# One down-projection sum per head, both branches' rows in one order on GpSimd, and piece two's token copies later: a hybrid decoder layer on one Trainium2 core

## The chip, the cores and the metric

The kernel runs on one core of one Trainium2 chip. The metric is device time in microseconds (us) of the whole program, less being better. An execution taken by the hardware profiler lies beside the timed runs; it gives when each engine was busy, what each instruction waited for, and which clock TensorE was granted. The engines are PE (TensorE), DVE (VectorE), ACT (ScalarE), POOL (GpSimd) and SP (SyncE, which here only issues DMAs). Each engine works its own instructions strictly in the order in which they were compiled: an instruction that waits holds everything behind it on that engine.

## The reference, cut to what matters

One layer, sequence 1024 plus 16 meta tokens, width 1024, all in float32. A token mixer has two parallel branches, gated linear attention (GLA, 4 heads) and mLSTM (4 heads), whose outputs are gated and merged; then comes a gated feed-forward network (FFN) with a causal convolution.

```python
proj = h @ w_in + b_in                        # q, k, v, gates of both branches
o_gla = head_rms(gla_chunked(...)) * silu(g_r)
o_ml  = head_rms(mlstm_chunked(...)) * sigmoid(m_o)
y = sigmoid(gate_a) * (o_gla @ w_branch_gla) + sigmoid(gate_b) * (o_ml @ w_branch_ml)
h = h + y @ w_out
u = causal_dwconv(rms_norm(h) @ w_up)
h = h + (silu(gate) * up) @ w_down
```

## The kernel before

Float32 operands are split on the chip into a high and a low part (ACT copies the high part, DVE subtracts it to get the low one), and each product is three matmuls: high x high, high x low, low x high. The large products of the gates and of the FFN use a Strassen-like scheme with seven block products instead of eight (`piece`), for which sums of token blocks and of weight blocks are made beforehand. The work around the change runs in four stages, in order of time.

**Heads (to about 680 us).** The loop at L950 goes over eight heads `s` (0 to 3 GLA, 4 to 7 mLSTM). Its main thread is the projections on PE (`value_proj`, `key_query_proj`); each of their steps calls `advance` (L931), which moves one generator of `closing` and one of `side` by a step. `side` holds `gla(s)` or `mlstm(s)`, the head's own recurrence. It ends in `rstd_of` (L88), whose power is taken on POOL (L93, tile `rs{s}r`). Its closing generator, `post(s)` (L558), scales the eight output blocks with that root on ACT (L563), transposes them on PE (L572), and stores two rows `of` to `oscm` or `oscg`. For s from 3 to 6, `post` then calls `token_sums(s - 3)` (POOL sums of token blocks, L464 and L469, stored by SP to `tsc`) and several `half_sums`.

`half_sums` (L478) is one of 22 pieces that make sums of w_down's blocks for the FFN's last product, long before they are needed. It takes one tile `ts`, loads 2 x 256 KB into it (L482, issued by POOL), makes four differences on POOL (L485) and stores two blocks to `tdn` (L487, POOL again). In the heads its tile is `gst` of pool `wp`, with one buffer, shared with `token_sums`' tile `tx` and with the rows `gb` of `merge_gate_b`. Heads make 2 + 3 + 3 of the 22, the gates 6, the first branch 3, the second branch 5.

**Gates (about 680 to 970 us).** `token_blocks` (L1071) loads the four token sums `T1` to `T4` from `tsc` with SP, in two pieces of columns (`W0` and the rest), and after each piece's loads come its splits on ACT (L1081) and DVE (L1082). Two further products, `merge_gate_b` for `COVER`, run on PE meanwhile. Then 13 pairs of gate products (L1124) run in two pieces each; pairs from 8 on also call `half_sums` (L1145) on tile `o0`. `gate_finish` multiplies a gate with a stored head output and stores the result to `otd`. The last plain product, `END`, is gate row 7 (`pe`), whose row `gb` goes to `gsc["b"]`.

**Branches (about 975 to 1200 us).** The first loop (L1206) makes `bg` = o_gla @ w_branch_gla in eight column tiles: `load_o("g")` (L1161) loads eight rows `ogL` of 513 KB with POOL, each split into `ogH` and `ogL` by ACT (L1171) and DVE (L1172); `merge_tile` (L1200) loads the gate rows `yg` with POOL; ACT takes their sigmoid (L1210), and DVE multiplies (L1213). At its second step it calls `load_o("m")`, which loads `omL` with SP, and three `half_sums`. The second loop (L1229) makes `bm` in eight tiles: it loads the row `sb` from `gsc["b"]` with SP (L1234), in two alternating tiles, ACT takes its sigmoid (L1235), DVE multiplies and adds (L1240, L1241), and while pieces are left each step ends in one `half_sums`, on the tile of the gate row that it has just used up.

**The rest:** the output product, the FFN's up products (with the convolution) and its down product.

The order on each engine is made by a compiler with a list scheduler: among the instructions that its own model calls ready it takes the one of highest priority, where priority is the order of the program, moved ahead by `hp(n)` blocks. So an instruction can be queued ahead of its place in the program. `tc.issue_after(x)` keeps the block's instructions on x's engine behind x, without a wait.

## Time and profile before

| | us |
|---|---|
| median of three runs | 1978.77 (1975.70 to 1982.41) |
| profiled execution | 1985.01 |
| its span, first to last instruction | 1983.3 |
| PE busy in it | 1883.7 |
| DVE busy | 1196.9 |
| ACT busy | 853.8 |
| POOL busy | 390.9 |

PE is busy for 95% of the span. A page of the profile gives each engine's busy time; the view of waits gives, for an engine and a line, who ended its idle time, with the total, the number of times and the longest; a timeline row gives start, duration, engine, line, operation, output<-inputs, shapes and count, and in brackets the idle time of the engine just before it and what ended it. SPq and ACTq rows are DMA issues.

### The profile page before, as it was taken

What the parts mean: (1) busy time and instruction counts of PE and PEld (TensorE: products, weight loads), DVE (VectorE), ACT (ScalarE), POOL (GpSimd) and SP (SyncE); (2) the same over time, 40 slices, a digit from 0 to 9 for tenths busy, and PEclk for the clock granted to TensorE, in tenths of its full rate; (3) what the DMA queues carried; (4) which work ended last, traced back from release to release, by engine and by line L of the source; (5) the groups of instructions that cost most, each with busy time, mean ns of one, the idle gap of its engine ahead of it and who ended that gap; (6) DMA issues with size and microseconds to landing.
All of it is one profiled execution on the core that took longest, in us unless ns stands there. A gap on an engine that the chain in (4) does not pass through costs nothing. (4 is left out here: it accounts for less than half of the span.)

```text
span 1983.3 us, 32663 instructions
## 1 busy us (share of the span) xinstructions
PE 1883.7 (95%) x13377; PEld 1799.7 (91%) x13377; DVE 1196.9 (60%) x1775; ACT 853.8 (43%) x1369; POOL 390.9 (20%) x425
## 2 busy tenths in 40 slices
PE   8999999999697989999869999999999999999998
PEld 8999989999686989999869999999999999987776
DVE  6555745655342255656251344788787878786867
ACT  5355554635333443432151123554444434354663
POOL 3101101142443001114340230012222222200000
PEclk8999999999898989999979999999999999999999
DMA  5111111143342547566871363333334333378794
GB/s 161 33 36 56 35 44 56 50 135 83 115 125 86 138 118 181 142 168 182 247 260 56 112 207 109 116 121 108 102 109 131 107 107 108 112 265 302 286 378 158
DMA packets 222593, 270.03 MB, mean 136 GB/s; under 512 B 13486, under 2 KB 176832, under 8 KB 222443
## 3 DMA queue, kind: packets, MB, share of 16 engines
q1 hardware_dynamic: 203771, 207.29, 33.8%
q0 software_dynamic: 14528, 50.39, 8.3%
q10 hardware_dynamic: 4144, 10.26, 1.5%
q8 instruction: 105, 1.72, 0.4%
q14 instruction: 45, 0.37, 0.1%
HBM read 198.33 MB, written 69.57 MB: 135 GB/s over the span
## 5 line engine op out<-in xcount | busy, mean ns | idle before, releaser
L485 POOL TENSOR_TENSOR ts<-ts 128x256 f32<-128x256 f32 x88 | 75.9, 866 | 69.2 <-DMA ts<-in_ffn_w_down_dram 66.7
L1188 PE MATMUL bg<-ogH,wH_bg 128*128 128x342 f32 x192 | 63.2, 330 | 24.3 <-ACT ogH L1171 24.3
L1372 POOL TENSOR_TENSOR SB<-SA,rg 128x512 f32<-128x512 f32 x20 | 32.1, 1604 | 237.1 <-issue 114.1
L201 PE MATMUL pv<-wH_mv,xH 128*128 128x256 f32 x256 | 75.5, 295 | 0.1
L201 PE MATMUL pv<-wH_gv,xH 128*128 128x256 f32 x256 | 75.3, 294 | 0.0
L1459 PE MATMUL po<-wH_wo,yH 128*128 128x256 f32 x256 | 72.6, 284 | 0.1
L201 PE MATMUL pv<-wL_mv,xH 128*128 128x256 f32 x256 | 72.5, 283 | 0.0
L201 PE MATMUL pv<-wH_mv,xL 128*128 128x256 f32 x256 | 72.5, 283 | 0.0
L1459 PE MATMUL po<-wL_wo,yH 128*128 128x256 f32 x256 | 71.9, 282 | 0.3 <-DVE wL_wo L107 0.3
L201 PE MATMUL pv<-wH_gv,xL 128*128 128x256 f32 x256 | 72.0, 281 | 0.0
L201 PE MATMUL pv<-wL_gv,xH 128*128 128x256 f32 x256 | 71.9, 281 | 0.0
L1459 PE MATMUL po<-wH_wo,yL 128*128 128x256 f32 x256 | 71.7, 281 | 0.0
L1407 DVE SCALAR_TENSOR_TENSOR cv<-u,fc,cv 128x1024 f32<-128x1024 f32 x44 | 65.3, 1485 | 0.4
L1188 PE MATMUL bg<-ogL,wH_bg 128*128 128x342 f32 x192 | 63.2, 330 | 0.3 <-DVE ogL L1172 0.3
L1188 PE MATMUL bg<-ogH,wL_bg 128*128 128x342 f32 x192 | 63.0, 328 | 0.0
L1354 POOL TENSOR_TENSOR A<-u2raw,A 128x512 fp32r<-128x512 f32 x20 | 44.0, 2198 | 93.0 <-ACT A L1353 93.0
L690 POOL TENSOR_TENSOR pk<-pk,kT 128x256 f32<-128x256 f32 (+1 forms) x24 | 29.5, 1231 | 163.5 <-ACT pk L688 163.5
L1188 PE MATMUL bm<-omH,wH_bm 128*128 128x342 f32 x192 | 61.4, 320 | 0.0
L1188 PE MATMUL bm<-omH,wL_bm 128*128 128x342 f32 x192 | 61.3, 319 | 0.0
L1188 PE MATMUL bm<-omL,wH_bm 128*128 128x342 f32 x192 | 61.2, 319 | 0.0
L1188 PEld LDWEIGHTS bg<-ogH,wH_bg 128*128 128x128 f32 x192 | 37.8, 197 | 24.9 <-ACT ogH L1171 24.9
L482 POOL DMA_DIRECT2D ts<-in_ffn_w_down_dram x44 | 32.0, 732 | 122.8 <-DVE yM L1244 84.3
(750 smaller groups left out, 7487.2 us busy)
## 6 DMA issues: line engine op xcount, KB each, us to landing
gw<-in_w_in_dram SPq DMA_DIRECT2D x26, 512.0 KB
ts<-in_ffn_w_down_dram POOLq DMA_DIRECT2D x44, 256.0 KB, 3.9
tdn<-ts POOLq DMA_DIRECT2D x44, 256.0 KB, 2.5
rg<-in_ffn_w_up_dram SPq DMA_DIRECT2D x22, 512.0 KB
ru<-in_ffn_w_up_dram SPq DMA_DIRECT2D x22, 512.0 KB
adr<-s SPq DMA_DIRECT2D x40, 256.0 KB
rd<-in_ffn_w_down_dram SPq DMA_DIRECT2D x20, 512.0 KB
do<-tdn SPq DMA_DIRECT2D x18, 512.0 KB
```

What stands on the lines that cost most here:

```text
L201: nc.tensor.matmul(pt[:, :DV], a[:, k, t0:t0 + P], b[:, k % 4, :], start=(i == 0), stop=(i == 3 * NK - 1))
L482: nc.gpsimd.dma_start(t[:, 2 * k:2 * k + 2], w_dn[P * (2 * m + k):P * (2 * m + k + 1), :].rearrange("p (i n) -> p i n", i=2)[:, :, 256 * c ...
L485: nc.gpsimd.tensor_tensor(t[:, o], t[:, a], t[:, b], OP.subtract)
L690: eng.tensor_tensor(e, e, k, OP.mult)
L1188: nc.tensor.matmul(pt[:, i, :n], a[:, k, :], b[k][:, t0:t0 + n], start=(k == 0 and j == 0), stop=(k == NK - 1 and j == 2))
L1354: eng.tensor_tensor(l, src, h.bitcast(F32), OP.subtract)
L1372: late.tensor_tensor(sb[:, 0:4], sa[:, 0:4], rg[:, 0:4], OP.subtract)
L1407: nc.vector.scalar_tensor_tensor(y, u[:, j:SEQ + j], fc[:, j, jj:jj + 1], y, OP.mult, OP.add)
L1459: nc.tensor.matmul(pt[:, :DV], a, b[:, k % 4, :], start=(k == 0 and i == 0), stop=(k == NK - 1 and i == len(terms) - 1))
```

## The change

`half_sums` is cut in two: `half_load` takes the tile and issues the two loads, `half_sums` makes the sums and stores. In `post`, heads 3 to 5 make one piece each instead of 2, 3 and 3: two generator steps after the token sums the load, three steps later the sums. The gates make 7 instead of 6 (two for pairs 8 and 9, one for 10 to 12), the first branch 6 instead of 3 (three at its third step, two at the fourth, one at the fifth), the second branch 6 instead of 5. `load_o` also returns its last load. The `om` loads go from SP to POOL, ordered behind the last `og` load. The `sb` loads go from SP to POOL, ordered behind the last `om` load, and the sigmoid of `sb` is ordered behind that of the last gate row of the first branch. The splits of the token sums become `token_splits(p)`: piece 0 where they were, piece 1 inside the first gate pair, after its second quarter.

```diff
--- before.py
+++ after.py
@@ -475,12 +475,16 @@
     tdn = [dram.tile([NP2, P, 2, 512], F32, name=f"tdn{i}") for i in range(2)]
     half = [(m, c) for m in range(NP2) for c in range(2)]
 
-    def half_sums(pool, tag, bufs=1):
+    def half_load(pool, tag):
+
         m, c = half.pop(0)
-        t = pool.tile([P, T], F32, name=f"ts{m}{c}", tag=tag, bufs=bufs)[:, :D].rearrange("p (i n) -> p i n", i=4)
+        t = pool.tile([P, T], F32, name=f"ts{m}{c}", tag=tag, bufs=1)[:, :D].rearrange("p (i n) -> p i n", i=4)
         for k in range(2):
             nc.gpsimd.dma_start(t[:, 2 * k:2 * k + 2], w_dn[P * (2 * m + k):P * (2 * m + k + 1), :].rearrange(
                 "p (i n) -> p i n", i=2)[:, :, 256 * c:256 * c + 256])
+        return t, m, c
+
+    def half_sums(t, m, c):
         for o, a, b in ((0, 1, 0), (1, 3, 1), (3, 3, 0), (2, 2, 3)):
             nc.gpsimd.tensor_tensor(t[:, o], t[:, a], t[:, b], OP.subtract)
         for i in range(2):
@@ -581,8 +585,13 @@
             yield
         if 3 <= s < 7:
             token_sums(s - 3)
-            for _ in range((2, 3, 3, 0)[s - 3]):
-                half_sums(wp, "gst")
+            if s < 6:
+                for _ in range(2):
+                    yield
+                t = half_load(wp, "gst")
+                for _ in range(3):
+                    yield
+                half_sums(*t)
 
 
 
@@ -1076,10 +1085,13 @@
         for c in (slice(0, W0), slice(W0, 514)):
             for i in (0, 2, 1, 3):
                 nc.sync.dma_start(TB[i][1][:, :, c].bitcast(F32), tsc[i].rearrange("k p c -> p k c")[:, :, c])
-            for i in (0, 2, 1, 3):
-                h, l = (t[:, :, c] for t in TB[i])
-                nc.scalar.activation(h, l.bitcast(F32), AF.Copy)
-                nc.vector.tensor_tensor(l, l.bitcast(F32), h.bitcast(F32), OP.subtract)
+
+    def token_splits(p):
+        c = (slice(0, W0), slice(W0, 514))[p]
+        for i in (0, 2, 1, 3):
+            h, l = (t[:, :, c] for t in TB[i])
+            nc.scalar.activation(h, l.bitcast(F32), AF.Copy)
+            nc.vector.tensor_tensor(l, l.bitcast(F32), h.bitcast(F32), OP.subtract)
 
     def gate_block(name, p):
         c0, n = W0 * p, (W0, W1)[p]
@@ -1114,6 +1126,7 @@
         return lambda t0: psG.tile([P, 512], F32, name=f"{name}_{t0}", tag=f"{'XYZ'[t0 // 342]}1")
 
     token_blocks()
+    token_splits(0)
     with hp(PRI_W):
         for _ in range(3):
             weights_step(0)
@@ -1137,12 +1150,14 @@
                 weights_step(q)
                 if q:
                     gate_finish(q - 1)
+                else:
+                    token_splits(1)
                 weights_step(q + 1)
             next(g)
             behind_ = g
         if q >= NK:
-            for _ in range(2 if q == NK else 1):
-                half_sums(gs, "o0")
+            for _ in range(2 if q < NK + 2 else 1):
+                half_sums(*half_load(gs, "o0"))
     next(behind_)
     for j in END:
         ugb[j] = u_cm(w_in, O_GB + P * j, f"gb{j}")
@@ -1167,10 +1182,10 @@
                 t[p, i] = pool.tile(shape, F32R, name=f"o{g}{p}{i}", tag=tag)
         for k in range(NK):
             h, l = (t[p, k // 4][:, k % 4, :NP] for p in "HL")
-            queue.dma_start(l.bitcast(F32), otd[g][k])
+            last = queue.dma_start(l.bitcast(F32), otd[g][k])
             nc.scalar.activation(h, l.bitcast(F32), AF.Copy)
             nc.vector.tensor_tensor(l, l.bitcast(F32), h.bitcast(F32), OP.subtract)
-        return tuple([t[p, k // 4][:, k % 4, :] for k in range(NK)] for p in "HL")
+        return tuple([t[p, k // 4][:, k % 4, :] for k in range(NK)] for p in "HL"), last
 
     ubg = [u_cm(w_bg, P * j, f"bg{j}") for j in range(NK)]
     ubm = [u_cm(w_bm, P * j, f"bm{j}") for j in range(NK)]
@@ -1202,7 +1217,7 @@
         nc.gpsimd.dma_start(yg[j], gsc["a"][j])
 
     merge_tile(0)
-    og = load_o("g", r2, "O", nc.gpsimd)
+    og, loaded = load_o("g", r2, "O", nc.gpsimd)
     for j in range(NK):
         y = yg[j]
         if j < NK - 1:
@@ -1212,10 +1227,10 @@
         with hp(PRI_E):
             nc.vector.tensor_tensor(th(y), pt, th(y), OP.mult)
         if j == 1:
-            with tc.issue_after(opened.ins):
-                om_ = load_o("m", r1b, "R", nc.sync)
-            for i in (5, 6, 7):
-                half_sums(r2, f"Y{i}")
+            with tc.issue_after(opened.ins), tc.issue_after(loaded.ins):
+                om_, loaded = load_o("m", r1b, "R", nc.gpsimd)
+        for i in ((), (), (5, 6, 7), (6, 7), (7,), (), (), ())[j]:
+            half_sums(*half_load(r2, f"Y{i}"))
 
     yH = [r2.tile([P, NK, 2, 256], F32R, name=f"yH{i}", tag=f"OH{i}") for i in range(2)]
     yL = [r2.tile([P, NK, 2, 256], F32R, name=f"yL{i}", tag=f"OL{i}") for i in range(2)]
@@ -1231,8 +1246,10 @@
             sb = r2.tile([P, T], F32, name=f"sb{j}", tag="hn", bufs=1)[:, :NP]
         else:
             sb = wp.tile([P, T], F32, name=f"sb{j}", tag="gst", bufs=1)[:, :NP]
-        nc.sync.dma_start(sb, gsc["b"][j])
-        nc.scalar.activation(sb, sb, AF.Sigmoid, bias=cc(C_GB + j))
+        with tc.issue_after(loaded.ins):
+            nc.gpsimd.dma_start(sb, gsc["b"][j])
+        with tc.issue_after(opened.ins):
+            nc.scalar.activation(sb, sb, AF.Sigmoid, bias=cc(C_GB + j))
         pt = prod3(ubm[j], om_, j < 1, f"bm{j}")
         with hp(PRI_E):
             for i in [slice(0, 3)] if j < NK - 1 else [slice(i, i + 1) for i in range(3)]:
@@ -1247,7 +1264,7 @@
                 nc.scalar.activation(yh, z, AF.Copy)
                 nc.vector.tensor_tensor(yL[i][:, j], z, yh.bitcast(F32), OP.subtract)
         if half:
-            half_sums(r2, f"Y{j if j < 3 else 3 - j % 2}")
+            half_sums(*half_load(r2, f"Y{j if j < 3 else 3 - j % 2}"))
     r1b_ctx.close()
     ps2_ctx.close()
     psF = ctx.enter_context(tc.tile_pool(name="psF", bufs=1, space=PSUM, reuse_waits="tile"))
```

## The prediction

> **What bounds the kernel now.** I read the page first, then the waits of PE, then the timelines of the engines around each of PE's long waits, then windows behind them for the clock. From the page and PE's waits, the four largest in their order:
>
> ```profile
> span 1983.3 us, 32663 instructions
> PE 1883.7 (95%) x13377; PEld 1799.7 (91%) x13377; DVE 1196.9 (60%) x1775; ACT 853.8 (43%) x1369; POOL 390.9 (20%) x425
> ```
>
> ```profile
> PE ot L572 <- ACT or L563: 28.6, 2, 15.2
> PE bg L1188 <- ACT ogH L1171: 24.3, 2, 16.6
> PE Xg L969 <- DVE gu L989: 8.2, 1, 8.2
> PE xtp L317 <- DVE xt L312: 4.3, 4, 2.8
> ```
>
> PE is busy 1883.7 of 1983.3 us, so the program is PE's work plus some 100 us in which PE has none. Three groups of waits hold 28.6 + 24.3 + 8.2 = 61.1 us of it in five long pieces; the next group has only 4.3. DVE, ACT and POOL are at 60% or less. The reading is therefore where each of the five ends, and whether the edit moves what ended it.
>
> Heads, two of the five. Rows of POOL, DVE, ACT and PE in order of time:
>
> ```profile
> 500.98 1.51 POOL L482 DMA_DIRECT2D ts<-in_ffn_w_down_dram  x2 [0.30 <-POOL xb L469]
> ...
> 511.98 0.69 POOL L487 DMA_DIRECT2D tdn<-ts  x1 [0.30 <-POOL ts L485]
> ...
> 513.70 0.17 DVE L91 TENSOR_SCALAR rs5v<-ss 128x9 f32<-128x9 f32 x1
> ...
> 529.69 2.32 POOL L485 TENSOR_TENSOR ts<-ts 128x256 f32<-128x256 f32 x3 [2.24 <-DMA ts<-in_ffn_w_down_dram]
> ...
> 533.26 1.92 POOL L93 TENSOR_TENSOR rs5r<-rs5v,mhalf 128x9 f32<-128x9 f32 x1
> ...
> 535.42 3.30 ACT L563 ACTIVATE or<-or,rs5r 128x256 f32<-128x256 f32 x8 [20.62 <-DVE rs5r L916]
> ...
> 535.98 1.68 PE L572 MATMUL ot<-ident,or 128*128 128x128 f32 x4 [15.19 <-ACT or L563]
> ```
>
> ```profile
> 582.05 0.70 POOL L487 DMA_DIRECT2D tdn<-ts  x1 [0.30 <-POOL ts L485]
> ...
> 585.37 0.15 DVE L91 TENSOR_SCALAR rs6v<-ss 128x9 f32<-128x9 f32 x1
> ...
> 603.02 1.90 POOL L93 TENSOR_TENSOR rs6r<-rs6v,mhalf 128x9 f32<-128x9 f32 x1
> ...
> 605.72 1.68 PE L572 MATMUL ot<-ident,or 128*128 128x128 f32 x4 [13.38 <-ACT or L563]
> ```
>
> The input of head 5's root, rs5v, is there at 513.87, but POOL takes the root at 533.26, because its queue holds three down sums, one after the other on one tile, and each waits for its own load (2.24 before the third). PE reaches the transposes at 535.98 - 15.19 = 520.79 and stands for 15.19. Head 6 is the same: input at 585.52, root at 603.02, PE stands for 13.38. The first down sum is done with its last store issue at 512.67 and at 582.75, each time ahead of the root's input; the second and third make the wait.
>
> Gates, one wait:
>
> ```profile
> 705.97 1.06 ACT L1081 ACTIVATE TH<-TL 128x1024 fp32r<-128x1024 f32 x1 [4.13 <-DMA TL<-tsc]
> ...
> 707.06 1.23 DVE L1082 TENSOR_TENSOR TL<-TL,TH 128x1024 fp32r<-128x1024 f32 x1 [3.96 <-ACT TH L1081]
> ...
> 713.78 0.42 DVE L989 TENSOR_TENSOR gu<-Xg,gu 128x258 f32<-128x258 f32 x1
> ...
> 714.25 0.58 PE L969 MATMUL Xg<-TH,gHSB 128*128 128x258 f32 x1 [8.16 <-DVE gu L989]
> ```
>
> PE wants to add into bank X, which DVE (L989) must have read before. ACT and DVE stand in their order on the last copy of the tokens' second piece, whose transfer ends at 705.97; nothing that PE wants at 706.09 needs that copy.
>
> First branch, two waits:
>
> ```profile
> 974.86 0.62 SPq L1234 DMA_DIRECT2D sb<-gscb  x1
> ...
> 994.73 1.15 ACT L1235 ACTIVATE sb<-sb,col 128x1026 f32<-128x1026 f32 x1 [18.27 <-DMA sb<-gscb]
> ...
> 1000.06 0.94 PE L1188 MATMUL bg<-ogH,wH_bg 128*128 128x342 f32 x2 [16.57 <-ACT ogH L1171]
> ...
> 1017.83 1.15 ACT L1235 ACTIVATE sb<-sb,col 128x1026 f32<-128x1026 f32 x1 [13.08 <-DMA sb<-gscb]
> ...
> 1115.18 1.23 DVE L1240 TENSOR_TENSOR sb<-bm,sb 128x1026 f32<-128x1026 f32 x1 [8.92 <-PE bm L1188]
> ...
> 1126.54 1.23 DVE L1240 TENSOR_TENSOR sb<-bm,sb 128x1026 f32<-128x1026 f32 x1 [5.71 <-PE bm L1188]
> ```
>
> ```profile
> 968.86 2.09 POOL L1170 DMA_DIRECT2D ogL<-otdg  x4 [5.17 <-ACT gu L996]
> 973.36 2.09 POOL L1170 DMA_DIRECT2D ogL<-otdg  x4 [2.40 <-ACT wH_bg L106]
> ...
> DMA to landing us min/median/max: 6.8/14.0/16.6
> ```
>
> The og loads are issued by 975.45 and, with 16.6 us at the longest from issue, have all landed by 974.92 + 16.6 = 991.5. But ACT, which must round them, sits 18.27 us on the sigmoid of sb0, a row of the other branch that DVE first multiplies at 1115.18, and then 13.08 on sb1's. PE stands 16.57 and then 24.3 - 16.6 = 7.7.
>
> After each wait PE runs at a lower granted clock (windows: PE's time, then the clock near the end of the row):
>
> ```profile
> 536.00:545.00 9.00, 9.00 (x39) 8.15 (x40) 2.96 (x5) 6.71 (x13) 0.00 (x0) 0.67 0.33 96
> 606.00:612.00 6.00, 6.00 (x32) 5.22 (x31) 2.10 (x5) 5.89 (x11) 0.00 (x0) 0.65 0.14 46
> 714.30:720.00 5.70, 5.70 (x29) 5.70 (x30) 0.85 (x2) 0.66 (x2) 0.00 (x0) 0.55 0.27 78
> 1000.00:1012.00 12.00, 11.62 (x56) 11.15 (x56) 6.92 (x6) 4.75 (x6) 3.37 (x5) 0.74 1.03 330
> 1020.00:1025.00 5.00, 5.00 (x22) 4.79 (x23) 5.00 (x3) 3.82 (x4) 4.75 (x7) 0.68 0.60 197
> ```
>
> Busy time x (1 - clock) is what each restart costs: 9.0 x 0.33 = 3.0, 6.0 x 0.35 = 2.1, 5.7 x 0.45 = 2.6, 11.6 x 0.26 = 3.0, 5.0 x 0.32 = 1.6: 12.3 us, which comes on top of the waits. [...]
>
> **The change, part by part.**
>
> *Heads.* Five down sums leave (8 to 3). One is left for each of heads 3 to 5, its load two steps after the token sums, its sums three steps later. By the rows above a single sum, even with POOL standing on its load, ended 1.0 us (513.70 - 512.67) and 2.6 us ahead of the root's input; that cover stays. Then root 1.92, 0.24 from its end (535.18) to ACT, and all of ACT's scaling, 3.30, give 513.87 + 5.46 = 519.3 against PE's 520.79, and 585.52 + 5.46 = 591.0 against 592.34: about 1.4 us in hand each time. Gain 15.19 + 13.38 + 3.0 + 2.1 = 33.7. What is late next: the load now waits two steps and then for the token stores that free its tile; if its sums slide behind the root's input, one sum's tail is exposed. Bounds 0 and two sums of 11.7 us (500.98 to 512.67); I take 2, nearest the hand of 1.0 us. Net 31.7.
>
> *Gates.* The four splits of piece two move behind the evacuation of X, so ACT and DVE reach L988 and L989 as PE delivers. Gain 8.16 + 2.6 = 10.8. They then lie before pair 0's second piece needs them. Four DVE splits at 1.23 are 4.9 us, and PE has X's last product and two more products first, 36 matmuls, by the window row above 36 x 5.70 / 29 x 0.55 = 3.9 us at full clock; since only the first two of the four are needed at once, between 0 and 1 us shows; I take 1. Net 9.8. One more down sum comes in this stage, costed under the branches.
>
> The down sums of the gates, two of six, on POOL:
>
> ```profile
> 940.44 1.44 POOL L482 DMA_DIRECT2D ts<-in_ffn_w_down_dram  x2 [3.61 <-DMA tdn<-ts]
> ...
> 954.06 1.44 POOL L482 DMA_DIRECT2D ts<-in_ffn_w_down_dram  x2 [4.61 <-DMA tdn<-ts]
> ```
>
> *Branches.* Both sb sigmoids leave the front of ACT's order, and the om loads leave the stretch in which og lands. PE can start at 1000.06 - 16.57 = 983.49. Then og's last row at 991.5, its split at 1.0 on ACT and 1.2 on DVE (the token copies above are of that size) and an eighth of a tile for PE (a tile is 1126.54 - 1115.18 = 11.36, so 1.4) end the first tile at 995.1; with nothing to wait for it would be 983.49 + 11.36 = 994.9. So transfers hide. Gain 16.57 + 7.7 + 3.0 + 1.6 = 28.9.
>
> Against it stands the seventh down sum of the gates. They follow each other on one tile every 954.06 - 940.44 = 13.6 us, so the last ends 13.6 later. If POOL's order has its sums ahead of the og loads, those issue at about 976 and not at 969 to 975: between 0 and 7 us. The order may put the loads first, as loads can be ready before sums; I take 4. Net 24.9. The om loads now follow og and a gate row on POOL, whose issue waits until row 7 of gate b is stored; behind it stand the om loads, the later gate rows and the sums. om is wanted when `bm` begins, at 995.1 + 7 x 11.36 = 1074.6, eighty us later, and the waiting gate row after three tiles. The 16 moved issues at 2.09 / 4 = 0.5 us cost POOL 8 us and free SP of as many. Six down sums at 11.7 to 13.6 us are 70 to 82 us on POOL beside eight tiles of 11.36 = 91, and the gate rows queue among them: hidden, if thinly. Behind the sigmoids on ACT are the weight splits, each made two tiles ahead (22.7 us).
>
> [...]
>
> *Sum.* 31.7 + 9.8 + 24.9 = 66.4. The profiled execution, 1985.01 (span 1983.3 and 1.7 around it), would come to 1918.6. It stands 6.2 above the median of the runs, 1978.77, so for the median I forecast 1978.8 - 66.4 = 1912.4.
>
> **Rivals.**
>
> *A: one head's wait stays.* The compiled order puts the sums of the load behind a later wait on POOL (it waits for stores of `of` rows there), and one root comes late as now. Gain 66.4 - 17 = 49, time 1930. For: single-buffered tile shared with three users. Against: the 1.0 and 2.6 us in hand.
>
> *B: the first branch gives part back.* ACT and DVE keep one order for og and om splits. If all eight om rows (at og's pace, 991.5 - 968.9 = 22.6 us for eight, from about 995) come ahead of the first tile's evacuation, that ends at 1017.6 + 3.5 = 1021, while PE wants the bank for its third tile at 995.1 + 22.7 = 1017.8; with the og loads 7 us late and a second restart the stage keeps about 10 of its 25. Time 1927.
>
> *C: the order hardly changes.* The scheduler keeps sums before roots and rows before splits, since its model does not see POOL stand. Gain under 6, time 1973 to 1979.
>
> *D: slower.* The transfers' view has the landing of a gate row:
>
> ```profile
> yg<-gsca POOLq DMA_DIRECT2D x8, 513.0 KB, 7.4
> ```
>
> GpSimd becomes the second branch's bound. The gate row sb of tile j+1 now queues on the same engine as the down sum that can start only when tile j is used up. In strict program order a tile takes two DVE steps of 1.23, one sum of 13.6, issue 0.6, landing 7.4 (yg's median) and sigmoid 1.15: 25.2 us, not the 11.36 between 1115.18 and 1126.54. Six tiles lose 6 x 13.8 = 83 us: 66.4 - 83 is 16 slower, 1995. It decides from 11.36 + 66.4 / 6 = 22.4 us a tile. For: POOL is in order. Against:
>
> ```profile
> 1003.43 0.52 SPq L1234 DMA_DIRECT2D sb<-gscb  x1
> ...
> 1120.86 0.34 SPq L1234 DMA_DIRECT2D sb<-gscb  x1
> ```
>
> sb1 was issued at 1003.43, far ahead of its program place, and the third row at 1120.86, as soon as its tile was free: rows are queued when ready, and with two alternating tiles row j+2, not j+1, is next to the sum of tile j.
>
> **How the numbers follow.** Forecast 0.64 (gain 56 to 77: 1902 to 1923; the top is every term without its deduction, 73.4, plus a small wait), A 0.10, B 0.12, C 0.05, D 0.09. About 0.3% (6 us) is what a measurement of this kernel can tell. Faster is the forecast, A, B and a little of C: 0.87; same 0.04; slower 0.09. The range 1901 to 1942 takes in forecast, A, B and both bounds of the unknown costs, and leaves out C and D. The predicted time is the forecast's, 1912.
>
> **What would show it.** Right: no wait of PE on `ot` over 2 us; the roots of heads 5 and 6 within 3 us of their inputs on POOL; L989 within 2 us of X's end in the first gate pair; ACT without an sb sigmoid before the last gate row's; the first `bg` matmul within 5 us of the last `pe`; windows behind these places at clock 1.00. Wrong: `ot` waits of over 10 us (A), ACT or DVE standing on om rows while PE waits for a bank (B), the same waits in their old places (C), or PE in `bm` waiting for DVE L1240 behind sb's landing (D).

## The result and the profile after

The changed kernel takes 1931.99 us (median of four runs, 1930.10 to 1936.24), the kernel before 1979.71 in the same comparison (1975.70 to 1982.41): 47.7 us less, a ratio of 0.9764 (95% interval 0.9739 to 0.9788). The profiled execution took 1930.77 us, 54.4 less in its span than the one before. The forecast was 1912 in a range of 1901 to 1942.

The page of the changed kernel, span and PE's line:

```profile
span 1928.9 us, 32657 instructions
PE 1872.7 (97%) x13377; PEld 1789.9 (93%) x13377; DVE 1196.0 (62%) x1775; ACT 854.5 (44%) x1369; POOL 399.6 (21%) x441
```

Four of PE's waits there (total, number, longest):

```profile
PE Xg L978 <- DVE gu L998: 5.7, 1, 5.7
PE po L1476 <- ACT wH_wo L106: 4.9, 1, 4.9
PE bg L1203 <- ACT ogH L1186: 3.9, 1, 3.9
PE ot L576 <- ACT of L578: 2.1, 1, 2.1
```

The wait of 28.6 us on `or` is gone, that on `ogH` fell from 24.3 to 3.9, that of bank X from 8.2 only to 5.7, and a new one of 4.9 stands at the output product (`po`). The 2.1 on `of` stood in before too. Line numbers have moved: L969 is now L978, L989 is L998, L1171 is L1186, L1235 is L1252.

Where the time went is read best by stages, cut at PE's first or last matmul of a kind (heads end at the start of the first `pc`, gates at that of the last `pe`, the first branch at the first `bm`, the second branch with the output product at the first `Yu`; up product to the first `pdV`, down product to the end). All twelve runs of the study are in the table; the parts add up to the span. Each ratio is to runs of the kernel before that were made beside it, whose medians lay between 1974.67 and 1979.71, so ratios compare better than medians; each row's stages are those of one profiled execution.

| kernel | median us | ratio to before | heads | gates | first branch | second branch, output | up | down |
|---|---|---|---|---|---|---|---|---|
| before | 1979.71 | 1 | 677.5 | 305.7 | 120.5 | 201.0 | 451.7 | 227.1 |
| after | 1931.99 | 0.9764 | 642.0 | 302.6 | 98.2 | 211.4 | 448.0 | 226.8 |
| tie_only | 1956.86 | 0.9889 | 677.4 | 302.4 | 97.9 | 202.4 | 449.3 | 226.2 |
| old_sums2 | 1961.42 | 0.9929 | 674.3 | 302.6 | 97.7 | 211.0 | 447.9 | 228.1 |
| sum_head6b | 1934.90 | 0.9797 | 649.5 | 301.5 | 97.6 | 208.8 | 448.0 | 225.7 |
| gate_tied2 | 1931.24 | 0.9779 | 642.5 | 301.7 | 98.0 | 211.1 | 447.9 | 227.4 |
| gate_order | 1924.79 | 0.9747 | 640.7 | 297.0 | 98.8 | 210.1 | 447.9 | 228.0 |
| sb_sync2 | 1922.56 | 0.9738 | 641.7 | 304.0 | 98.1 | 201.4 | 450.3 | 227.3 |
| om_sync | 1925.79 | 0.9754 | 643.1 | 302.0 | 100.2 | 201.9 | 448.2 | 229.0 |
| og_first | 1928.37 | 0.9766 | 640.8 | 302.9 | 96.7 | 211.9 | 447.7 | 226.7 |
| all_three | 1917.51 | 0.9704 | 644.7 | 295.4 | 95.7 | 207.8 | 448.0 | 226.9 |
| best | 1922.38 | 0.9717 | 642.4 | 297.3 | 98.4 | 201.0 | 447.8 | 226.4 |
| best_head2 | 1915.14 | 0.9683 | 641.3 | 294.9 | 95.5 | 201.0 | 447.5 | 227.1 |
| after_again | 1931.56 | 0.9763 | 644.6 | 305.6 | 98.5 | 211.1 | 447.9 | 227.4 |

So the change gave 35.5 us in the heads and 22.3 in the first branch, lost 10.5 in the second branch and the output product, and the rest is 3.2 in the gates and 3.9 in the FFN. Those last two are not the change's: after_again, the same program, has 305.6 in the gates as before had, and tie_only, whose gates are those of before, has 302.4; in the FFN nothing was changed, and before's own execution stood 5 us above its median. What is left, 35.5 + 22.3 - 10.5 = 47.3, is close to the 47.7 of the medians. That it is so close is partly luck: the heads, which nine of the kernels have in common (after, gate_tied2, gate_order, sb_sync2, om_sync, og_first, all_three, best, after_again), took 640.7 to 644.7 us, so a figure of the heads from one execution can be off by up to 4.

**Heads.** GpSimd's timeline, the down sum of head 4 from its load to its last store, then the roots of heads 5 and 6:

```profile
502.06 1.51 POOL L483 DMA_DIRECT2D ts<-in_ffn_w_down_dram  x2 [0.61 <-POOL xb L469]
...
512.10 0.69 POOL L491 DMA_DIRECT2D tdn<-ts  x1 [0.30 <-POOL ts L489]
...
514.08 1.83 POOL L93 TENSOR_TENSOR rs5r<-rs5v,mhalf 128x9 f32<-128x9 f32 x1 [1.16 <-DVE rs5v L91]
...
566.45 1.85 POOL L93 TENSOR_TENSOR rs6r<-rs6v,mhalf 128x9 f32<-128x9 f32 x1 [2.88 <-DVE rs6v L91]
```

Each root now waits only for its input from DVE (the bracket names `rs5v` and `rs6v`), and the sum ahead of rs5r ends at 512.79, 1.0 us before DVE starts on that input (513.82): the hand of 1.0 that the prediction read from before.

**Gates.** ACT, DVE and PE at the first gate pair:

```profile
668.02 1.06 ACT L1093 ACTIVATE TH<-TL 128x1024 fp32r<-128x1024 f32 x1 [3.26 <-DMA TL<-tsc]
...
669.77 1.06 ACT L1036 ACTIVATE gHA<-gw 128x1024 fp32r<-128x1024 f32 x1 [0.35 <-DMA gw<-in_w_in_dram]
...
672.52 0.39 ACT L997 ACTIVATE gu<-Vg 128x258 f32<-128x258 f32 x1 [0.40 <-ACT gb L453]
...
675.80 0.42 DVE L998 TENSOR_TENSOR gu<-Xg,gu 128x258 f32<-128x258 f32 x1
...
676.27 0.58 PE L978 MATMUL Xg<-TH,gHSB 128*128 128x258 f32 x1 [5.69 <-DVE gu L998]
```

The copies of piece two (L1093) stand in ACT's order where they stood, ahead of the evacuation L997, and wait 3.26 for their transfer. The program's line moved, the compiled order did not. Between that copy and L998 DVE also has six operations on weights, from 670.87 to 675.80; what they mean is shown with gate_tied2.

**First branch.** ACT and PE from the last `pe` (it ends at 944.81) to the first `bg`:

```profile
944.74 1.06 ACT L106 ACTIVATE wH_bg<-wr_bg 128x1024 fp32r<-128x1024 f32 x1 [3.23 <-PE pe L158]
...
945.70 0.44 ACT L453 ACTIVATE gb<-pe 128x342 f32<-128x342 f32 x1
...
946.55 1.15 ACT L1225 ACTIVATE yg<-yg,col 128x1026 f32<-128x1026 f32 x1 [0.41 <-ACT gb L453]
947.60 1.99 ACT L1186 ACTIVATE ogH<-ogL 128x1026 fp32r<-128x1026 f32 x2
...
948.70 0.94 PE L1203 MATMUL bg<-ogH,wH_bg 128*128 128x342 f32 x2 [3.89 <-ACT ogH L1186]
```

No `sb` sigmoid is here any more. What is left is a row of ACT work: a weight split that had to wait for PE to free its slot, the last evacuation of `pe`, the gate row's sigmoid, and only then `ogH`. Row og0 had landed at 947.15, 0.45 us before that.

**Second branch.** GpSimd, ACT and PE from the down sum of the fourth tile to the output product:

```profile
1096.12 1.44 POOL L483 DMA_DIRECT2D ts<-in_ffn_w_down_dram  x2 [2.11 <-DMA tdn<-ts]
...
1101.00 1.50 POOL L489 TENSOR_TENSOR ts<-ts 128x256 f32<-128x256 f32 x1 [3.44 <-DMA ts<-in_ffn_w_down_dram]
...
1109.73 0.57 POOL L1250 DMA_DIRECT2D sb<-gscb  x1
...
1114.83 1.16 ACT L1252 ACTIVATE sb<-sb,col 128x1026 f32<-128x1026 f32 x1 [14.37 <-DMA sb<-gscb]
...
1138.25 1.15 ACT L1252 ACTIVATE sb<-sb,col 128x1026 f32<-128x1026 f32 x1 [6.46 <-DMA sb<-gscb]
1139.31 1.04 ACT L106 ACTIVATE wH_wo<-wr_wo 128x1024 fp32r<-128x1024 f32 x1
...
1140.40 0.58 PE L1476 MATMUL po<-wH_wo,yH 128*128 128x256 f32 x1 [4.87 <-ACT wH_wo L106]
```

Row sb5 is issued at 1109.73, behind a down sum whose load was issued at 1096.12 and waited for (3.44), and half of the next. ACT stands 14.37 us on its sigmoid, the delay runs through sb6 and sb7 (6.46), and behind sb7's sigmoid stands the weight split that PE needs: 4.87 us, and 1.5 in three smaller waits. Windows behind the three waits (PE's time, granted clock third from the end):

```profile
676.30:682.00 5.70, 5.70 (x32) 5.70 (x33) 0.85 (x2) 0.78 (x2) 0.00 (x0) 0.63 0.29 80
949.00:955.00 6.00, 5.68 (x24) 5.24 (x24) 3.18 (x3) 2.71 (x3) 0.02 (x1) 0.62 1.03 322
1140.50:1150.00 9.50, 8.36 (x42) 7.55 (x42) 8.17 (x15) 3.56 (x7) 1.06 (x2) 0.60 0.56 176
```

The last costs 8.36 x 0.40 = 3.3 us of clock; with 6.4 of waits that is 9.7 of the 10.5.

### The profile page after: what moved, and what is told of

It reads as the page before. It is cut to its first block, busy times and chain, and to the rows that moved or that the text cites. A ratio compares the mean times of both kernels' runs of the same rounds, so it can differ in the third digit from the quotient of the medians.

```text
span 1928.9 us, 32657 instructions
## 1 busy us (share of the span) xinstructions
PE 1872.7 (97%) x13377; PEld 1789.9 (93%) x13377; DVE 1196.0 (62%) x1775; ACT 854.5 (44%) x1369; POOL 399.6 (21%) x441
## 5 line engine op out<-in xcount | busy, mean ns | idle before, releaser
L1476 PEld LDWEIGHTS po<-wH_wo,yH 128*128 128x128 f32 x256 | 49.3, 193 | 7.1 <-ACT wH_wo L106 5.1
L1713 POOL TENSOR_TENSOR fr<-fv,mhalf 128x1 f32<-128x1 f32 x8 | 6.4, 805 | 229.6 <-DVE fv L1711 229.6
```

What stands on the lines that cost most here:

```text
L1476: nc.tensor.matmul(pt[:, :DV], a, b[:, k % 4, :], start=(k == 0 and i == 0), stop=(k == NK - 1 and i == len(terms) - 1))
```

## The experiments

Theory after the comparison: the heads' gain is the number of sums ahead of the root, the first branch's gain is the sigmoids' place on ACT, the second branch's loss is the row loads' place on GpSimd, and the gates' edit did nothing. Rivals: the down sums' number and the transfers.

**tie_only: one line of the change, on the kernel before.**

```diff
-        nc.scalar.activation(sb, sb, AF.Sigmoid, bias=cc(C_GB + j))
+        with tc.issue_after(opened.ins):
+            nc.scalar.activation(sb, sb, AF.Sigmoid, bias=cc(C_GB + j))
```

> The kernel before with one edit: the sigmoid of sb is ordered behind the last of the first branch's gate rows on ACT. Loads, queues and down sums stay as before. Theory after om_sync (whose first branch, from the last pe to the first bm, took 100.2 us against 98.2 in the changed kernel and 120.5 before): the sigmoids' place on ACT holds PE, the loads' order is worth 2. Expected: 20 us less than before, ratio 0.990. Rival: with om and sb on Sync and three down sums the og rows land late without the change's order, and 5 to 10 of the 20 stay: ratio 0.992 to 0.995.

Measured: ratio 0.9889 (0.9864 to 0.9914), 21 us. PE's waits:

```profile
PE ot L572 <- ACT or L563: 28.1, 2, 14.9
PE Xg L969 <- DVE gu L989: 5.1, 1, 5.1
PE bg L1188 <- ACT ogH L1171: 3.9, 1, 3.9
```

The first branch takes 97.9 us, not more than in the changed kernel: its whole gain is had by this order alone, and the loads' queue and the down sums added nothing to it on balance. The wait on bank X is 5.1 here and was 8.2 in before, with the same order of gate instructions.

**old_sums2: the change without its new distribution of down sums.**

```diff
-            if s < 6:
-                for _ in range(2):
-                    yield
-                t = half_load(wp, "gst")
-                for _ in range(3):
-                    yield
-                half_sums(*t)
+            for _ in range((2, 3, 3, 0)[s - 3]):
+                half_sums(*half_load(wp, "gst"))
...
-            for _ in range(2 if q < NK + 2 else 1):
+            for _ in range(2 if q == NK else 1):
...
-        for i in ((), (), (5, 6, 7), (6, 7), (7,), (), (), ())[j]:
+        for i in (5, 6, 7) if j == 1 else ():
```

> The changed kernel with the down sums of before: 2, 3, 3 in the heads with load and sums together, 6 in the gates, 3 in the first branch, 5 in the second; the loads' queues, the sigmoid's order and the splits' place stay as changed. Theory: the heads' two waits with their restarts come back, 35 us, while the first branch gets its 6 us back; the second branch has sb behind sums still, with one sum less, 0 to 5 less loss: 1932 + 35 - 6 - 2 = 1959. Rival: the heads' gain came from elsewhere than the number of sums, 1926 to 1935. Rival on the second branch: the sixth sum alone makes its loss, then 10 go: 1951.

Measured 1961.42, ratio 0.9929 (0.9912 to 0.9946):

```profile
PE ot L576 <- ACT or L567: 26.6, 2, 14.6
PE po L1471 <- ACT wH_wo L106: 4.1, 1, 4.1
PE bg L1198 <- ACT ogH L1181: 3.9, 1, 3.9
```

The heads' waits are back (stage +32.4). The first branch did not get its 6 us, with six sums in the gates as before, and the second branch loses its 10 with five sums too. So neither guess that blamed a sum alone holds: the wait on `ogH` is 3.9 here, in tie_only and in the changed kernel alike, and the sixth sum is not what the second branch pays for.

**sum_head6b: the seventh sum of the gates into head 6.**

```diff
-            if s < 6:
+            if s < 7:
...
-            for _ in range(2 if q < NK + 2 else 1):
+            for _ in range(2 if q == NK else 1):
```

> The changed kernel with the seventh down sum of the gates moved to head 6 (heads 4, gates 6). Theory: that sum on GpSimd holds the og loads back; they issue at 939.5 and would issue about 9 us earlier, so the wait of 3.89 us for ogH at the first bg matmul, the small ones behind it (0.55) and part of the 6 us at clock 0.62 (2.3) go: 1932 - 6 = 1926. Rival: the og rows are limited by their transfers (DMA share 1.0 from 944 to 965), which start earlier but compete as before, gain under 2: 1930 to 1933. Second rival: the sum in head 6 delays head 7's root and costs up to 12: 1938.

Measured 1934.90, ratio 0.9797 (0.9781 to 0.9813), the second rival's side, but not by its mechanism. ACT's timeline, first in the tail of the heads, then before the first `bg`:

```profile
632.97 1.15 ACT L453 ACTIVATE gb<-pj 128x342 f32<-128x342 f32 x3 [2.42 <-DMA tdn<-ts]
...
951.28 1.06 ACT L106 ACTIVATE wH_bg<-wr_bg 128x1024 fp32r<-128x1024 f32 x1 [3.23 <-PE pe L158]
...
953.09 1.15 ACT L1225 ACTIVATE yg<-yg,col 128x1026 f32<-128x1026 f32 x1 [0.40 <-ACT gb L453]
954.15 7.69 ACT L1186 ACTIVATE ogH<-ogL 128x1026 fp32r<-128x1026 f32 x8
```

The root was not late. The sum holds the tile `gst`, into which `merge_gate_b` evacuates its row; ACT waits 2.42 for the sum's store, PE 4.5, and the heads end 7.6 later than in the changed kernel (4.8 later than in any of the nine kernels with its heads). And although og0 landed at 943.19, eight us before PE was done with `pe`, its split comes at 954.15, behind the same row of ACT work as in the changed kernel.

**gate_tied2, then gate_order: the copies forced behind the evacuation, then the next pair's weights too.**

```diff
+            read[0] = nc.scalar.activation(g1, V[:, :n], AF.Copy)
+            read[1] = nc.vector.tensor_tensor(g1, X[:, :n], g1, OP.add)
...
+                    with tc.issue_after(read[0].ins), tc.issue_after(read[1].ins):
+                        token_splits(1)
```

> The changed kernel with one thing more: the four ACT and four DVE splits of piece two are ordered behind the evacuation of banks V and X on each engine. Theory: moving the splits in the program did not move them on ACT and DVE, whose compiled order still has them ahead of that evacuation; there lie PE's 5.69 us of waiting at 670.59 and a restart at clock 0.63 for 5.7 us (2.1 us). Expected: the wait is gone, 1932 - 7.8 = 1924. Rival: the splits are needed soon after by piece two, or their last transfer is late, and the wait only moves there: 1930 to 1934.

Measured 1931.24, ratio 0.9779 (0.9764 to 0.9795): no gain. PE's wait and the ACT row that made it:

```profile
PE Xg L978 <- DVE gu L1000: 4.8, 1, 4.8
```

```profile
669.42 1.06 ACT L1038 ACTIVATE gHA<-gw 128x1024 fp32r<-128x1024 f32 x1 [7.32 <-DMA gw<-in_w_in_dram]
```

With the copies gone, the next thing in ACT's order, a weight split of the second pair, waits 7.32 for its own transfer. DVE stands 9.05 on the same split, then makes six operations on weights from 670.51 to 675.45, and only then L1000, the evacuation for which PE waits. The same order stood in the profile of before:

```profile
707.76 1.06 ACT L1027 ACTIVATE gHA<-gw 128x1024 fp32r<-128x1024 f32 x1 [0.39 <-DMA gw<-in_w_in_dram]
...
708.85 1.23 DVE L1028 TENSOR_TENSOR gLA<-gw,gHA 128x1024 fp32r<-128x1024 f32 x1 [0.56 <-ACT gHA L1027]
```

The weight's transfer ended there at about 707.7, 1.8 us behind that of the last copy (705.97), and DVE had the same six operations from 708.85 up to L989 at 713.78. Five of them are the second pair's (in gate_order they come behind the evacuation); one (`gLSB`) belongs to the weights that PE is about to use. gate_order ties `weights_step(1)`, all weight operations of the second pair, in the same way:

> The changed kernel; the token splits of piece two and, besides, all weight splits of the second gate pair are ordered behind the evacuation of banks V and X in the first. Theory after gate_tied2: a second layer stood behind the first; there ACT waited 7.32 us at 669.42 for the next pair's weight (gHA) with the evacuation behind it, and DVE 9.05. Expected: Xg's wait of 4.8 to 5.7 us and its restart (2) go: 7 to 8 below the changed kernel, ratio to before near 0.973. Rival: what the evacuation waits for is gHSB, PE's own operand, which needs the first pair's weight; then PE waits as long under another name, ratio 0.976.

Measured 1924.79, ratio 0.9747 (0.9734 to 0.9760); the gates take 297.0, and PE's wait on bank X is gone. DVE's row and the windows:

```profile
672.77 0.69 DVE L1056 TENSOR_TENSOR gS<-gw,gw 128x512 f32<-128x512 f32 x1 [5.83 <-DMA gw<-in_w_in_dram]
```

```profile
664.00:674.00 10.00, 9.68 (x82) 9.47 (x80) 2.88 (x4) 7.18 (x11) 0.00 (x0) 1.00 0.89 193
674.00:684.00 10.00, 8.61 (x69) 8.40 (x70) 9.48 (x14) 1.58 (x3) 0.00 (x0) 1.00 0.01 2
```

Behind the evacuation DVE's order has a subtraction of the second pair's weights ahead of the token differences; it waits 5.83 for its transfer, and PE waits 1.0 for the first of them and 0.7 for an evacuation behind them. Some 5.5 and not 7.8 were gained against the 302.6 of the first profile. In the four kernels with gate_order's order the gates take 294.9 to 297.3, in all others 301.5 to 305.7, so the gain is clear of the spread, though its size is known to a few us only. The wait of 1.0 us leaves the clock at 1.00.

**sb_sync2: rows sb2 to sb7 from Sync.**

```diff
-        with tc.issue_after(loaded.ins):
-            nc.gpsimd.dma_start(sb, gsc["b"][j])
+        if j < 2:
+            with tc.issue_after(loaded.ins):
+                nc.gpsimd.dma_start(sb, gsc["b"][j])
+        else:
+            nc.sync.dma_start(sb, gsc["b"][j])
```

> The changed kernel with the gate rows sb2 to sb7 of the second branch loaded by Sync instead of GpSimd (sb0 and sb1 stay). Theory: on GpSimd they stand behind down sums that wait for their own transfers; sb5 issues at 1109.73, lands 1114.74, and ACT and DVE lag from there until wH_wo comes 4.87 us late for the output product (6.4 us of waits in all, and 9.5 us at clock 0.60, 3.8). Expected: those waits are gone, 1932 - 10 = 1922. Rival: the lag comes from the extra down sum itself (DVE and GpSimd slow each other, transfers compete) and the row's queue matters little: 1930 to 1933.

Measured 1922.56, ratio 0.9738 (0.9718 to 0.9757). sb5's load on Sync, its sigmoid on ACT, and the window at the output product:

```profile
1097.86 0.33 SPq L1253 DMA_DIRECT2D sb<-gscb  x1
```

```profile
1102.78 1.16 ACT L1255 ACTIVATE sb<-sb,col 128x1026 f32<-128x1026 f32 x1 [5.75 <-DMA sb<-gscb]
```

```profile
1135.00:1145.00 10.00, 9.83 (x84) 9.62 (x83) 7.79 (x17) 5.06 (x13) 1.07 (x2) 1.00 0.79 249
```

Counted from the first `bm`, sb5 goes out at 54.0 instead of 67.1 us, 13 earlier. No PE wait is left at the output product, its clock is 1.00, and the stage takes 201.4 instead of 211.4: the loss of the second branch is these rows' place in GpSimd's queue. From sb5's issue to its sigmoid it is 4.92 us on Sync and was 5.10 on GpSimd, so the landing itself is not what changed. That DVE and GpSimd slow each other shows in the changed kernel, but is small: at 1101.82 DVE's L1258 takes 1.76 us beside a GpSimd difference of 1.50 (0.72 to 0.99 in the ones after it), and 1.22 in the other tiles. The ratio is better than the changed kernel's by 0.0026 (5 us) only, and the two intervals overlap; against gate_tied2, in the same comparison and with a second branch of 211.1, it is 8.7 us less (1922.56 and 1931.24), with intervals apart.

**om_sync: om and all sb rows on Sync, the sigmoids' order kept.**

```diff
-            with tc.issue_after(opened.ins), tc.issue_after(loaded.ins):
-                om_, loaded = load_o("m", r1b, "R", nc.gpsimd)
+            with tc.issue_after(opened.ins):
+                om_, loaded = load_o("m", r1b, "R", nc.sync)
...
-        with tc.issue_after(loaded.ins):
-            nc.gpsimd.dma_start(sb, gsc["b"][j])
+        nc.sync.dma_start(sb, gsc["b"][j])
```

> The changed kernel with om and all sb rows loaded by Sync again; the order of the sb sigmoid behind that of the last gate row is kept. It separates the two edits of the first branch. Theory that the sigmoid's place on ACT made the gain: the first branch keeps its 22 us, and with sb on Sync the second branch loses nothing: as sb_sync2, ratio 0.974. Theory that the loads' order made it: sb0, sb1 and the first om rows issue from Sync before og has landed, some ten rows at 1.45 us compete with og's eight, and the first bg tile ends 4 to 12 us later: ratio 0.976 to 0.980.

Measured 1925.79, ratio 0.9754 (0.9740 to 0.9767), between the two by the ratio; the stages speak for the first theory. The second branch takes 201.9, so it loses next to nothing. The first branch takes 100.2, 2.0 more than in the changed kernel, and in tie_only, with the same loads on Sync, 97.9. So ordering om behind og on GpSimd is worth 0 to 2 us.

**og_first, all_three, best, best_head2: what is left, put right.** og_first puts the first three `og` splits ahead of the third weight split and the gate row's sigmoid (`prep` puts a weight split behind `behind[0]`, here that of bg2):

```diff
+            with hp(PRI_E) if g == "g" and k < 3 else nullcontext():
+                a = nc.scalar.activation(h, l.bitcast(F32), AF.Copy)
+            if g == "g" and k == 2:
+                behind.append(a)
...
+        with tc.issue_after(behind[0].ins) if behind else nullcontext():
+            opened = nc.scalar.activation(y, y, AF.Sigmoid, bias=cc(C_GA + j))
```

> The changed kernel; ACT's split of the third bg weight and the sigmoid of the first gate row are ordered behind the first three og splits. Theory after sum_head6b and old_sums2: the 3.9 us before the first bg is a row of ACT work after PE's last pe (weight split 1.06, which waits for PE to free its slot, evacuation 0.44, sigmoid 1.15, then the og split 0.96), the same in all kernels whether og landed 8 us earlier or not. Expected here, with og0 landing at 947.15: the wait shrinks only to about 3.3 (landing, split, first matmul), gain 0.5 to 2. Rival: the transfers alone set it, no gain.

Measured 1928.37, ratio 0.9766 (0.9753 to 0.9780): the first branch falls by 1.5 to 96.7, too little for the ratio to show. PE's wait fell from 3.9 to 2.0 and not to 3.3, because og0 landed earlier in this execution than in the changed kernel's: at 943.71, 0.28 us before the last `pe` ended.

all_three joins sb_sync2, gate_order and og_first and moves the seventh down sum of the gates to the end of the second branch:

```diff
-            for _ in range(2 if q < NK + 2 else 1):
+            for _ in range(2 if q == NK else 1):
...
-            half_sums(*half_load(r2, f"Y{j if j < 3 else 3 - j % 2}"))
+            half_sums(*half_load(r2, f"Y{j if j < 3 or j == 6 else 3 - j % 2}"))
```

> The changed kernel with sb2 to sb7 on Sync, the gate order of gate_order, the ACT order of og_first, and the seventh down sum of the gates moved to the end of the second branch (7 there, 6 in the gates). Expected by the theories: sb 10, gates 7, first branch 2 to 4 (og0 lands before pe ends, left are the evacuation 0.44 and the split): 19 to 21 below the changed kernel in the profile, ratio to before 0.966 to 0.969. Rival: parts of it are taken up later, in the down product or by the seventh sum holding a residual row's tile: 0.970 to 0.973.

Measured 1917.51, ratio 0.9704 (0.9687 to 0.9722), within the rival's range. Gates and first branch came as expected, but the second branch takes 207.8, so a seventh sum there gives back 6 of its 10. Its trace has part of them where the changed kernel had its loss: PE waits 1.4, 0.9 and 1.0 us at the start of the output product (`wH_wo`, `wL_wo`, `yH`). best therefore leaves the sums where the change had them:

> The changed kernel with sb2 to sb7 on Sync, the gate order and the ACT order of og_first, and all down sums where the change put them (7 in the gates, 6 in the second branch). Theory after all_three (whose second branch with 7 sums, first bm to first Yu, took 207.8 us against 201.4 in sb_sync2): the seventh sum there took 6 back. Expected: gates 5.5, first branch 1.5, second branch 10: 17 below the changed kernel, ratio to before 0.968. Rival: what all_three lacked is lost elsewhere, ratio 0.970 as there.

Measured 1922.38, ratio 0.9717 (0.9693 to 0.9741), the rival's number. In its profiled execution, the fastest of five at 1914.92, the second branch has its 201.0, but the first branch is back at 98.4. ACT's row says why:

```profile
942.82 1.06 ACT L1200 ACTIVATE ogH<-ogL 128x1026 fp32r<-128x1026 f32 x1 [2.37 <-DMA ogL<-otdg]
```

With the ACT work moved out of its way, `ogH` now waits 2.37 us for og0. GpSimd has the og loads behind the seventh sum's stores:

```profile
934.01 0.69 POOL L491 DMA_DIRECT2D tdn<-ts  x1 [0.30 <-DMA gscb<-gu]
...
935.25 2.68 POOL L1198 DMA_DIRECT2D ogL<-otdg  x5
```

Two limits of about the same length lie on each other: in the changed kernel og0 landed at 947.15, and ACT's row let its split go at 947.60. old_sums2 and sum_head6b took away the sum and saw the ACT row. og_first and best took away the row, and there the sum shows in the one execution and not in the other: og0 landed 0.28 us before the last `pe` ended in og_first, 2.84 behind it in best. Over all profiled kernels with seven sums in the gates og0 landed between 2.8 us before that end and 3.0 behind it, in those with six, before among them, 7.8 to 10.5 before it. best_head2 takes away both, with the seventh sum in head 2, which has no token sums:

```diff
         if 3 <= s < 7:
             token_sums(s - 3)
-            if s < 6:
+        if 2 <= s < 6:
...
-            for _ in range(2 if q < NK + 2 else 1):
+            for _ in range(2 if q == NK else 1):
```

> best with one edit: the seventh down sum of the gates becomes a sum of head 2 (heads 4, of heads 2 to 5; gates 6; second branch 6). It undoes the second of two limits that lay on each other at the first bg. In best, with the ACT order mended, og0 lands at 942.80, 2.84 us after the last pe ends, behind that sum, and PE still waits 4.0; in all_three, with 6 sums, the wait was 2.0. Theory: og0 lands before pe ends, PE waits 2.0, the first branch takes 95.7 us against 98.4, and nothing else changes: 2.5 below best, ratio 0.969. Rival: head 2 has its sum where a root is made, and the heads lose as in sum_head6b, 5 to 7: ratio 0.974.

Measured 1915.14, ratio 0.9683 (0.9661 to 0.9704): 16.4 us below the changed kernel's median (1931.56), and its interval lies below that one's. PE's wait, ACT's row and the window behind:

```profile
PE bg L1219 <- ACT ogH L1200: 2.0, 1, 2.0
```

```profile
937.40 2.96 ACT L1200 ACTIVATE ogH<-ogL 128x1026 fp32r<-128x1026 f32 x3 [0.40 <-ACT gb L453]
```

```profile
938.50:942.00 3.50, 2.81 (x10) 2.53 (x11) 3.50 (x4) 3.50 (x4) 0.00 (x0) 0.61 1.03 400
```

`ogH` waits for nothing but ACT, the first branch takes 95.5, and the heads stay at 641.3. PE's wait is 2.0, as in og_first, so what moving the sum adds is that og0 is there in good time, 8.0 us before the last `pe` ends; how often it comes late with the sum in the gates was not counted. The 7 us between the medians of best and best_head2 are more than the 2.9 of this stage, and their ratios' intervals overlap.

after_again is the changed kernel once more, as a base for tie_only and best:

> The changed kernel as it is, on the chip of the two others, as their base. Expected: ratio 0.976 as at first, its gates (first pc to last pe) 302.5 us, first branch 98.2, second branch with output product 211.4. Rival: parts of these are of one execution only, and differ by over 1 us.

Measured 1931.56, ratio 0.9763 (0.9741 to 0.9786). First branch (98.5) and second branch (211.1) repeat within 0.3 us. The heads do not, 644.6 instead of 642.0, nor do the gates, 305.6 with a wait of 8.2 on bank X instead of 5.7: the rival's case. That wait ends with a transfer, and it lay between 4.7 and 8.2 in all executions whose order holds it.

## Why the prediction was right, and where it was not

The sign was right and the range held, but the sum of the gains was 18.7 us too high: 66.4 forecast, 47.7 measured. The 1932 us lie outside the forecast's own 1902 to 1923, beside the times of rivals A (1930) and B (1927), and neither of these happened: both roots are made on time, and PE waits for no bank behind om rows. The range was drawn wide enough for A and B, and other losses of that size filled it; so far the hit is luck. Of the signs, the roots, the sigmoids and the first `bg` came out right; L998 is not within 2 us of bank X's end, and the clock behind bank X and the first `bg` is 0.63 and 0.62, not 1.00. By its steps:

- **Heads, forecast 31.7, measured 35.5 in the stage, 32.4 against old_sums2.** The mechanism is shown: sums behind the first held the roots. The 2 us set aside for a load that slides were not needed; without them the term was 33.7, and the 3.8 between forecast and stage are within what the heads differ by from one execution to the next.
- **Gates, forecast 9.8, measured nothing.** The step that failed is "ACT and DVE reach L988 and L989 as PE delivers". The edit moves the copies in the program, and the compiled order kept them ahead of the evacuation, as rival C had it for the whole change. The premise "nothing that PE wants needs that copy" was right, but the wait was two deep, and the second layer stood in the profile of before: the second pair's weights, whose transfer ended 1.8 us behind the last copy's, and 4.9 us of DVE's work on weights. gate_tied2 moved the copies and gained nothing, gate_order moved the second pair's weights behind as well and gained 5.5. The 3.2 us between the two first profiles are the spread of one transfer.
- **First branch, forecast 24.9, measured 22.3.** That the sigmoids held ACT is shown by tie_only alone. The term of 28.9 let no wait stand, and there it failed: PE waited 3.9 us at the first `bg`, 0.6 in two smaller waits, and lost 2.2 to the clock behind, 6.7 in all, which is the difference to 22.3. The 3.9 came from a row of ACT work that the prediction did not list among what stands ahead of `ogH`, with the seventh sum close under it. So the deduction of 4 named a true limit (best), but that it came near the measured number is luck. The sign "within 5 us of the last `pe`" was met for both reasons.
- **Second branch, forecast 0, measured -10.5.** The failed step is "hidden, if thinly". Rival D named the mechanism and its place and was priced as a rate of all tiles, 25.2 us each; the `bm` tiles kept their 11.36 until the fifth (DVE's multiplications from 1054.21 to 1099.54 in four steps of 11.33), and the loss came from one row, sb5, 13 us late, through ACT's order into the next stage. The rows cited against D showed rows queued as soon as they were ready on Sync, which has no sums in its queue; on GpSimd readiness did not help sb5 behind a sum that stood 3.44 us on its own load. A rival between 0 and 83 us was missing.
- **Sum of the errors:** 9.8 in the gates, 10.5 in the second branch, 2.6 in the first branch, and 3.8 to the good in the heads make 19.1.

The queue that issues the loads counts here for sb, at 10 us (second branch 211.4 and 201.4), and not by the time to landing (4.92 us from issue to sigmoid on Sync, 5.10 on GpSimd) but by what stands ahead in the queue; for om it does not show, since om_sync was 2.0 slower in that stage. The lower clock behind the changed kernel's three waits, 5.70 us at 0.63, 5.68 at 0.62 and 8.36 at 0.60, loses 2.1 to 3.3 each, against 1.6 to 3.0 behind the five of before.

**Open.** The executions of best and best_head2 spread over 12 and 9 us, and the profiled one is the shortest of each; where the others spend more was not seen in a trace. Why a seventh sum in the second branch makes the rows late even when Sync loads them was not followed further.

## What to carry to other kernels

Find the instruction that holds an in-order queue, and then ask what the queue would stand on next: here, in two places, an edit that removed the first holder gained nothing, because a second of about the same length lay under it (bank X: a wait of 5.7 us, then 4.8 in gate_tied2; the first `bg`: 3.9, then 4.0 in best). A line moved in the program moved nothing here, where a scheduler orders the queue by its own idea of what is ready; tie the order and look at it on the engine (gate_order gained 5.5 us so). A load that somebody waits for does not belong on a queue whose other work waits for loads of its own: on GpSimd sb5 went out 13 us later than on Sync, and the stage was 10 us longer.

## What was not expected of the hardware

In the changed kernel the length of a wait of about 2 us did not tell whether the granted clock fell. PE waits 2.10 us before 390.87, 2.15 before 601.19, 2.21 before 1266.90 and 2.59 before 1699.14; windows of 6 us behind the first two:

```profile
390.80:396.80 6.00, 5.93 (x39) 5.73 (x40) 2.94 (x6) 5.10 (x8) 0.00 (x0) 1.00 0.71 188
601.20:607.20 6.00, 6.00 (x24) 5.28 (x25) 1.70 (x6) 2.85 (x11) 0.00 (x0) 0.72 0.54 175
```

Behind the third it is 0.72 again (1266.90 to 1272.90), behind the fourth, the longest, 1.00 (1699.10 to 1705.10). A wait of 1.0 us left the clock at 1.00 (gate_order, 674 to 684 us), and one of 2.0 was followed by 3.5 us at 0.61 (best_head2, at the first `bg`).

The same instructions in the same order also waited 5.1 or 8.2 us on bank X from one execution to the next (tie_only and before), 5.7 or 8.2 in the changed kernel, so a term of 3 us that ends in a transfer cannot be read from one profile.
